# Two score banks in place of the attention's output bank in the first block's output projection

## The chip, the cores and the metric

One NeuronCore of one Trainium2 chip runs the whole program. The metric is device time in microseconds (us) of one execution; the number that counts is the median of several runs. Matmuls accumulate in PSUM, which this kernel uses as eight banks, numbered 0 to 7, each of 128 partitions by 512 float32 values.

## The reference, cut to what matters

Two transformer blocks are applied one after the other to 512 tokens of width 1024, all in float32. The change lies in the first block, and there between these lines:

```python
mixed = jnp.concatenate([out_a.reshape(b, s, A_Q_W), out_b.reshape(b, s, B_W)], axis=-1)
x = x + jnp.einsum('bse,ed->bsd', mixed, w_out)          # the output projection
hn = rmsnorm(x, mlp_norm_g)
hid = jnp.square(jax.nn.relu(jnp.einsum('bsd,df->bsf', hn, w_up)))
x = x + jnp.einsum('bsf,fd->bsd', hid, w_down)
```

`out_a` is a sliding-window attention of eight heads, `out_b` a "forgetting" attention of eight heads; `w_out` is 1024 x 1024, `w_up` 1024 x 4096. The second block (modulation by a conditioning vector, pooling and neighbourhood attention, another MLP) follows.

## The kernel before

**Arithmetic.** Every float32 matrix product is made of three passes over operands that are split into a high and a low part (`split`, lines 149 to 152: ScalarE copies the high part, VectorE subtracts to get the low one; `mm3`, lines 154 to 158: high by high, high by low, low by high). In the profile these are the rows of lines 156, 157 and 158.

**Who sets the order.** The kernel is written in program order, and a scheduler that goes by simulated times makes one fixed list of instructions for each engine from it: an instruction that comes later in the program moves ahead of one whose inputs are late in the simulation. On the chip each engine works through its list in order and waits at the first instruction that is not ready. Tiles of the same tag wait for one another: a new tile in a PSUM bank may be written once the last reader of the tile before it is done.

**Banks.** `banks` (line 146) gives each kind of tile a ring of banks, and `ps` (line 140) hands them out in turn. The first attention has `x=(0, 1)` for projections, `o=(2,)` for the attention's weighted sums, `t=(3, 4, 7)` for transposes and `s=(5, 6)` for scores (line 289). The output projection has `a=A1` and `t=(3, 4)` (line 294), with `A1 = (0, 1, 2)` (line 91). Behind it, line 950 sets `a=(0, 1, 2)`, `t=(3, 4)`, `s=(5, 6, 7)` for the MLP, and line 852 lengthens the ring `s` by `MORE = (0, 1)` until the sixth "up" tile: up tiles 0 to 4 lie in banks 5, 6, 7, 0, 1.

**Attention tail.** `attn_b` (line 666) takes two heads at a time (four pairs). Scores go to a ring `s` bank (lines 676 to 684), VectorE takes the maximum (line 687), ScalarE the exponential (line 689), which is the bank's last reader. The probabilities are transposed (line 707), split, multiplied with the values into bank 2 (`values`, line 712, matmuls of line 581), and `mixed` (line 583) splits bank 2 into `mixT`, the transposed input of the output projection. Counted through the program (1 tile in `gates`, 16 in `attn_a`, 32 in `attn_b`), the ring's last score tile lies in bank 5 and the one before it in bank 6.

**Output projection.** `out_proj` (line 757) goes over two halves of the output columns; in each, `token_major` (line 794) fetches and splits four weight tiles (kp 0 to 3, two k-blocks of 128 each; `o1w00` to `o1w03` for the first half, `o1w10` to `o1w13` for the second) and goes over four token tiles of 128 tokens. Here they are called h0t0 to h0t3 and h1t0 to h1t3. A token tile is 24 matmuls of 128x512 into one bank: 18 for kp 0 to 2 and 6 for kp 3. All token tiles of one kp use the same weight tile, and five weight tiles fit at once (`PARTS = 5`), so `o1w11` takes the place of `o1w00` and can be split only when h0t3 has used that. With three banks in turn, h0t0 to h0t3 are in banks 0, 1, 2, 0 and h1t0 to h1t3 in 1, 2, 0, 1. kp 3 of a token tile is put behind the transposes of the tile two before it (lines 816 and 817).

**After each token tile** `evac1` (line 940) adds the bank to `xa` (line 942, VectorE), multiplies by the norm's gain (`xg`, line 944: GpSimd in the first half, VectorE in the second), transposes on TensorE (line 220; in the trace `n_0t` to `n_3t`), and splits the result into `hT`, the input of the MLP: the first half of the columns makes k 0 to 3 of `hT`, the second k 4 to 7.

**Beside it** `mods` (line 874) computes the second block's modulation rows on VectorE: `macc` (lines 900 and 902, 128x1024 each), fed by 512 KB transfers of `mod`. It begins behind a sigmoid of the conditioning vector, whose exponential (line 883) runs on ScalarE.

**MLP up.** `up` (line 832) makes one 128-wide slice of the hidden layer; for the first five (`NSP = 5`) the 512 tokens go in two halves of 256, each of 24 matmuls (eight k, three passes), so that the first 24 need only the token tiles 0 and 1. Its low weight parts come from GpSimd for the first four slices (`WPJ = 4`).

Of the kernel before, what the change touches and what calls it, by code (L numbers as in the profile page):

```python
# [87 lines left out]
NSP = 5  # L88
MORE = (0, 1)
EARLY = (2, 1)  # L90
A1 = (0, 1, 2)
XR = (3, 5, 7)
A2 = (0, 1, 5, 2, 6)
S2 = (5, 6, 7)
# [39 lines left out]
class Build:  # L134
# [132 lines left out]
    def run(self):  # L267
        tc, nc, a = self.tc, self.nc, self.a
        with ExitStack() as es:
# [21 lines left out]
            with ExitStack() as both:  # L291
                self.xc = both.enter_context(tc.tile_pool(name="xc", bufs=1, reuse_waits="tile"))
                with ExitStack() as ph:
                    self.banks(a=A1, t=(3, 4))
                    self.xp = ph.enter_context(tc.tile_pool(name="xp", bufs=1, reuse_waits="tile"))
# [1255 lines left out]
```

## Time and profile before

| | |
|---|---|
| median of 3 runs | 1253.91 us (1253.65 to 1258.92) |
| the profiled execution's own time | 1258.2 us |
| its span | 1256.4 us |
| busy: TensorE, VectorE, ScalarE, GpSimd | 1211.0, 843.2, 594.2, 256.4 us |
| mean granted TensorE clock | 0.987 |

The span is the profiler's, from the first to the last instruction; the execution's own time is 1.8 us longer. In the profile PE is TensorE, DVE VectorE, ACT ScalarE, POOL GpSimd. A row of a timeline gives start, duration, engine, line, operation, output<-inputs, shape and count, and in brackets how long the engine stood idle before it and what ended that. The duration of a matmul is longer than the spacing to the next one, since matmuls overlap; spacing is what counts. A row of a table of stretches gives for each engine its busy time and number of instructions, then the granted clock as a share of full speed (PEclk), the DMA engines' busy share and GB/s.

The stretch of the change runs from the end of the first attention, at about 230 us, over the output projection to the first "up" slices of the MLP at about 291 us.

### The profile page before, as it was taken

How to read it: one execution, taken by the hardware profiler on the slowest of the kernel's cores; microseconds unless marked ns; L12 is line 12 of the kernel's file. 1: busy time of each engine (PE TensorE's matmuls, PEld its weight loads, DVE VectorE, ACT ScalarE, POOL GpSimd, SP SyncE). 2: the span in 40 equal slices, each digit the busy share in tenths (PEclk: the TensorE clock that was granted, in tenths of full speed). 3: DMA queues.
4: the chain of work that ended last, by engine and by line, in shares of the span. 5: the costliest groups of instructions: out<-in, count | busy, mean ns of one | idle time of the engine just before them, and what ended most of it. 6: DMA issues, size and time to landing. Idle time of an engine off the chain costs nothing. (4 is left out here: it accounts for less than half of the span.)

```text
span 1256.4 us, 16975 instructions
## 1 busy us (share of the span) xinstructions
PE 1211.0 (96%) x6304; PEld 1013.8 (81%) x6304; DVE 843.2 (67%) x1461; ACT 594.2 (47%) x1103; POOL 256.4 (20%) x324
## 2 busy tenths in 40 slices
PE   7899999998999999999999999999899999999997
PEld 6898888788888878888889878777798888888775
DVE  3798776497988864346355557574867568578675
ACT  5576655434323313225245546463566454453442
POOL 2787552243010000000013224030600000000000
PEclk8998999999999999999999999999999999999998
DMA  6221222355668744234145311315355535436331
GB/s 165 64 59 46 66 63 68 101 167 149 206 217 258 235 138 141 67 101 135 67 151 158 85 51 53 102 38 201 119 189 161 166 86 177 142 98 187 101 101 67
DMA packets 154154, 155.42 MB, mean 124 GB/s; under 512 B 14489, under 2 KB 115624, under 8 KB 154072
## 3 DMA queue, kind: packets, MB, share of 16 engines
q1 hardware_dynamic: 149096, 143.08, 37.4%
q0 software_dynamic: 4400, 10.22, 2.6%
q8 instruction: 49, 0.80, 0.3%
q10 hardware_dynamic: 576, 1.05, 0.2%
q14 instruction: 33, 0.27, 0.1%
HBM read 147.96 MB, written 6.36 MB: 123 GB/s over the span
## 5 line engine op out<-in xcount | busy, mean ns | idle before, releaser
L902 DVE SCALAR_TENSOR_TENSOR macc<-mod,silu_c,macc 128x1024 f32<-128x1024 f32 x56 | 76.7, 1379 | 14.1 <-DMA mod<-in_w_mod_dram 14.1
L1453 POOL TENSOR_TENSOR ss<-ss,nhalf 128x1 f32<-128x1 f32 x4 | 3.0, 740 | 332.8 <-DVE ss L1452 332.8
L1305 DVE TENSOR_TENSOR m2d<-m2d,m2d 128x1024 f32<-128x1024 f32 x28 | 34.1, 1222 | 21.9 <-DMA m2d<-in_w_mlp_out_dram 21.8
L979 DVE SCALAR_TENSOR_TENSOR xa<-m1d,r,xa 128x512 f32<-128x512 f32 x32 | 23.8, 746 | 35.3 <-PE m1d L158 35.3
L151 ACT ACTIVATE m1hid<-m1sq 128x512 fp32r<-128x512 f32 x32 | 20.0, 630 | 37.4 <-DVE m1sq L848 37.4
L922 POOL DMA_DIRECT2D modrows<-mrow x8 | 3.9, 492 | 144.4 <-DVE mrow L920 90.2
L152 DVE TENSOR_TENSOR npl<-t,nph 128x512 fp32r<-128x512 f32 x32 | 21.7, 680 | 16.4 <-ACT nph L151 16.3
L152 DVE TENSOR_TENSOR m1hid<-m1sq,m1hid 128x512 fp32r<-128x512 f32 x32 | 21.9, 686 | 9.1 <-ACT m1hid L151 9.1
L185 POOL TENSOR_SCALAR w<-w,g_attn 128x384 f32<-128x384 f32 x20 | 25.6, 1290 | 8.9 <-DMA w<-in_w_in_dram 6.3
L687 DVE TENSOR_REDUCE mb<-sb 128x1 f32<-128x128 f32 (+3 forms) x32 | 15.6, 486 | 16.7 <-PE sb L684 16.6
L198 POOL TENSOR_SCALAR p<-p,d 128x512 f32<-128x512 f32 x8 | 14.0, 1752 | 55.8 <-DVE d L1120 26.5
L1119 ACT ACTIVATE p<-s,m 128x512 f32<-128x512 f32 x32 | 22.0, 689 | 5.8 <-DVE m L1117 5.8
L689 ACT ACTIVATE pb<-sb,mb 128x128 f32<-128x128 f32 (+3 forms) x32 | 16.8, 526 | 15.8 <-DVE mb L687 15.5
L847 ACT ACTIVATE m1re<-m1up 128x512 f32<-128x512 f32 x32 | 18.7, 583 | 11.0 <-PE m1up L158 11.0
L156 PE MATMUL pj<-w_0h,xnT 128*128 128x384 f32 (+1 forms) x48 | 18.5, 386 | 4.5 <-ACT pjs L411 3.3
L151 ACT ACTIVATE nph<-t 128x512 fp32r<-128x512 f32 x32 | 19.1, 596 | 7.4 <-PE t L1130 7.2
L1073 POOL TENSOR_TENSOR tb<-G,nam 128x256 f32<-128x256 f32 x24 | 17.8, 774 | 22.3 <-DVE m L1113 12.5
L848 DVE SCALAR_TENSOR_TENSOR m1sq<-m1up,m1re 128x512 f32<-128x512 f32 x32 | 21.8, 682 | 0.0
L1270 ACT ACTIVATE m2sq<-m2up 128x512 f32<-128x512 f32 x32 | 18.7, 584 | 6.5 <-PE m2up L158 6.5
L1331 DVE TENSOR_TENSOR y<-m2p,y 128x512 f32<-128x512 f32 x32 | 21.1, 682 | 0.2 <-PE m2p L158 0.2
L1272 ACT ACTIVATE m2sq<-m2sq 128x512 f32<-128x512 f32 x32 | 20.2, 633 | 0.9
L151 ACT ACTIVATE pbh<-tb 128x128 fp32r<-128x128 f32 (+3 forms) x32 | 13.7, 435 | 14.5 <-PE tb L707 14.4
(2045 smaller groups left out, 4624.3 us busy)
## 6 DMA issues: line engine op xcount, KB each, us to landing
m2d<-in_w_mlp_out_dram SPq DMA_DIRECT2D x53, 512.0 KB, 3.7
mod<-in_w_mod_dram SPq DMA_DIRECT2D x48, 512.0 KB, 4.4
m1u<-in_w_up_dram SPq DMA_DIRECT2D x32, 512.0 KB, 4.4
m1d<-in_w_down_dram SPq DMA_DIRECT2D x32, 512.0 KB, 3.6
m2u<-in_w_mlp_in_dram SPq DMA_DIRECT2D x32, 512.0 KB, 4.1
w<-in_w_in_dram SPq DMA_DIRECT2D x16, 512.0 KB, 4.0
w<-in_w_in_dram SPq DMA_DIRECT2D x48, 128.0 KB, 2.6
o1w<-in_w_out_dram SPq DMA_DIRECT2D x8, 512.0 KB, 3.7
```

Of the source, the lines that this page charges most:

```text
L151: self.nc.scalar.activation(out=hi, in_=src, func=AF.Copy)
L152: (eng or self.nc.vector).tensor_tensor(out=lo, in0=src, in1=hi.bitcast(F32), op=ALU.subtract)
L185: eng.tensor_scalar(out=rv[:, i], in0=rv[:, i], scalar1=g, scalar2=None, op0=ALU.mult)
L847: ac(out=r, in_=acc, func=AF.Relu)
L848: nc.vector.scalar_tensor_tensor(out=s, in0=acc, scalar=0.0, in1=r, op0=ALU.max, op1=ALU.mult)
L902: nc.vector.scalar_tensor_tensor(out=accs[s], in0=rw, scalar=sc[:, s, k:k + 1], in1=accs[s], op0=ALU.mult, op1=ALU.add)
L979: nc.vector.scalar_tensor_tensor(out=x[t][:, cols], in0=acc, scalar=r2[:, t:t + 1], in1=x[t][:, cols], op0=ALU.mult, op1=ALU.add)
L1119: ac(out=pr, in_=s, func=AF.Exp, bias=m[:, 2:3], accum_out=den[:, 0:1])
L1270: ac(out=s, in_=acc, func=AF.Relu)
L1272: ac(out=s, in_=s, func=AF.Square)
L1305: tt(out=o, in0=x, in1=z, op=ALU.subtract)
L1331: tt(out=Y[n][tau], in0=acc, in1=Y[n][tau], op=ALU.add)
```

## The change

The ring of the first block's output projection is made of the banks 0, 1, 5 and 6, four in place of three. Nothing else is edited. h0t0 to h0t3 then lie in banks 0, 1, 5, 6 and h1t0 to h1t3 in 0, 1, 5, 6 again; bank 2 is not used between the attention's last weighted sum and the MLP. The up tiles stay in banks 5, 6, 7, 0, 1.

```diff
-A1 = (0, 1, 2)
+A1 = (0, 1, 5, 6)
```

## Rows read from the trace of the kernel before

**Rows 1.** The page's busy times: engine, busy us, share of the span, instructions.

```profile
PE 1211.0 (96%) x6304; PEld 1013.8 (81%) x6304; DVE 843.2 (67%) x1461; ACT 594.2 (47%) x1103; POOL 256.4 (20%) x324
```

**Rows 2.** Stretches: busy time by engine, granted clock, DMA share, GB/s.

```profile
core 0: us, PE busy (x) PEld busy (x) DVE busy (x) ACT busy (x) POOL busy (x), PEclk, DMA share, GB/s
230.00:240.00 10.00, 8.90 (x61) 7.12 (x60) 6.64 (x18) 5.48 (x13) 2.03 (x4) 1.00 0.18 55
...
242.00:247.00 5.00, 4.93 (x15) 3.91 (x16) 1.31 (x2) 0.00 (x0) 2.52 (x2) 0.66 1.02 319
247.00:278.00 31.00, 31.00 (x145) 25.18 (x144) 26.11 (x28) 11.55 (x16) 10.44 (x8) 1.00 0.53 161
278.00:291.00 13.00, 9.07 (x58) 8.57 (x58) 13.00 (x12) 4.14 (x6) 12.68 (x8) 0.87 0.62 189
291.00:440.00 149.00, 149.00 (x742) 125.11 (x741) 125.38 (x136) 52.16 (x67) 14.98 (x26) 1.00 0.67 213
```

**Rows 3.** TensorE's waits from 230 to 291 us: us, times, longest.

```profile
PE n_2t L220 <- DVE xg L944: 3.9, 1, 3.9
PE o L156 <- DVE mixT L152: 1.9, 1, 1.9
PE tb L707 <- DVE db L690: 0.9, 1, 0.9
```

**Rows 4.** Timeline of TensorE, 239 to 253 us.

```profile
239.87 0.34 PE L581 MATMUL ob<-pbh,vb3l 128*64 128x128 f32 x2
242.07 0.47 PE L156 MATMUL o<-o1w00h,mixT 128*128 128x512 f32 x1 [1.87 <-DVE mixT L152]
...
247.90 0.39 PE L156 MATMUL o<-o1w00h,mixT 128*128 128x512 f32 x1
...
252.09 0.60 PE L220 MATMUL n_0t<-ident,xg 128*128 128x128 f32 x4
```

**Rows 5.** Timeline of ScalarE, 233 to 252 us.

```profile
233.90 0.69 ACT L689 ACTIVATE pb<-sb,mb 128x512 f32<-128x512 f32 x1
...
249.49 1.06 ACT L151 ACTIVATE o1w11h<-o1w 128x1024 fp32r<-128x1024 f32 x1 [8.01 <-PE o L158]
...
251.86 0.20 ACT L883 ACTIVATE silu_e<-silu_c 128x16 f32<-128x16 f32 x1
```

**Rows 6.** Timeline of VectorE, 250 to 290 us.

```profile
250.59 1.23 DVE L152 TENSOR_TENSOR o1w11l<-o1w,o1w11h 128x1024 fp32r<-128x1024 f32 x1 [7.28 <-ACT o1w11h L151]
...
279.08 0.68 DVE L942 TENSOR_TENSOR xa<-o,xa 128x512 f32<-128x512 f32 x1
279.68 6.31 DVE L902 SCALAR_TENSOR_TENSOR macc<-mod,silu_c,macc 128x1024 f32<-128x1024 f32 x2
285.91 0.68 DVE L944 TENSOR_TENSOR xg<-xa,g_mlp 128x512 f32<-128x512 f32 x1
...
288.91 0.68 DVE L152 TENSOR_TENSOR hT<-n_1t,hT 128x512 fp32r<-128x512 f32 x1
289.51 0.68 DVE L942 TENSOR_TENSOR xa<-o,xa 128x512 f32<-128x512 f32 x1
```

**Rows 7.** Timeline of TensorE, 278 to 291 us.

```profile
278.06 0.28 PE L156 MATMUL m1up<-hT,m1u0h 128*128 128x256 f32 x1
...
282.52 0.29 PE L157 MATMUL m1up<-hT,m1u1h 128*128 128x256 f32 x1
286.74 0.63 PE L220 MATMUL n_2t<-ident,xg 128*128 128x128 f32 x4 [3.93 <-DVE xg L944]
287.12 0.39 PE L158 MATMUL m1up<-hT,m1u1l 128*128 128x256 f32 x1
...
290.85 0.28 PE L157 MATMUL m1up<-hT,m1u0h 128*128 128x256 f32 x1
290.97 0.28 PE L158 MATMUL m1up<-hT,m1u0l 128*128 128x256 f32 x1
```

**Rows 8.** Timeline of GpSimd, 279 to 285 us.

```profile
279.22 2.41 POOL L152 TENSOR_TENSOR m1u1l<-m1u,m1u1h 128x1024 fp32r<-128x1024 f32 x1
281.59 3.32 POOL L152 TENSOR_TENSOR m1u2l<-m1u,m1u2h 128x1024 fp32r<-128x1024 f32 x1
```

**Rows 9.** Instructions writing macc, 256 to 284 us: ns min/median/max, starts, form.

```profile
L902 DVE SCALAR_TENSOR_TENSOR macc<-mod,silu_c,macc x12: 1272/1284/3358, 258.5 to 282.6; 128x1024 f32<-128x1024 f32 x12
```

## The prediction

> **What bounds the kernel now.** I began with the page's busy times: TensorE is busy for 96% of the span [rows 1], so time is only to be had where TensorE waits or where its clock is low. The table of stretches then says where that is. From 291 to 440 us TensorE is busy for all 149 us at full clock [rows 2]: whatever is won or lost before 291 us is carried through that stretch unchanged. From 230 to 291 us there are three losses: a low busy time before 242 us, a granted clock of 0.66 from 242 to 247 us, and 9.07 busy of 13.00 us from 278 to 291 us, at a clock of 0.87 [rows 2]. From 247 to 278 us TensorE is full at full clock.
>
> The list of waits names the gaps: 1.9 us for VectorE's `mixT`, 0.9 us in the last softmax, 3.9 us for `xg` before the transposes `n_2t` [rows 3]. The timeline shows the first of them: after the attention's last weighted sum (matmuls `ob` at 239.87) TensorE stands 1.87 us, until h0t2 begins at 242.07 [rows 4]. That wait is the bank's. h0t2's first 18 matmuls use kp 0 to 2, made of other heads, finished long before; but h0t2 sits in bank 2, and bank 2 still holds the weighted sum that `mixed` reads. h0t3, in bank 0, comes behind it. The clock falls just after this gap, to about half (1.2 of 2.4 GHz): the 18 matmuls of h0t2 take 247.90 - 242.07 = 5.83 us, the next 18, h0t3's, 252.09 - 247.90 = 4.19 us [rows 4].
>
> The last gap has another cause. From 278 to 291 us VectorE is busy for 13.00 of 13.00 us [rows 2]; it is the late engine there, and TensorE fills its time with up slices until 282.52, then waits until 286.74 for `n_2t`, whose input `xg` VectorE began only at 285.91 [rows 6, 7].
>
> **The change part by part.**
>
> *No wait for bank 2.* h0t2 moves to bank 5, h0t3 to bank 6. The last reader of bank 5 is the last exponential, at 233.90 + 0.69 = 234.6 us [rows 5]; bank 6 is free a score tile earlier. So from 234.6 us on h0t2's 18 matmuls, and h0t3's 18, can fill any hole: 36 matmuls at 4.19 / 18 = 0.233 us are 8.4 us of work, more than every hole before 242 us together. Gain: the 1.87 us. The 0.9 us wait in the softmax lies around 234 us, at the edge of the time at which the bank comes free, and whether the scheduler's list has a matmul there isn't to be seen: 0 to 0.9 us, and I take 0.
>
> *The clock.* Without the gap the matmuls behind it should keep the full clock, as they did around the 0.9 us wait: the stretch 230 to 240 us has 8.90 busy of 10.00 and a clock of 1.00 [rows 2]. Gain: 5.83 - 4.19 = 1.64 us; bounds 0 (the clock falls anyway) and 1.64. I take 1.64, for between full busy and a 0.9 us hole no row shows a fall.
>
> The Trainium skill ("TensorE: Matmul & The Clock Gate", section "A second HAM failure mode: psum-queue depth-cycling") blames a falling clock on going round through banks with short pauses. By that rule the 1.64 us would not come back and the gain here would be 1.87 us alone. The trace speaks against it: three banks are gone round from 247 to 278 us at a clock of 1.00 with no hole [rows 2].
>
> *Does it reach the later work?* ScalarE's split of `o1w11` at 249.49 waited 8.01 us for TensorE to be done with `o1w00`, which h0t3 uses last; VectorE's half of that split follows at 250.59 after 7.28 us of idling; and the exponential that lets the `macc` work begin stands in ScalarE's list behind it, at 251.86 [rows 5, 6]. If h0t3's first matmuls come 1.87 + 1.64 = 3.5 us sooner, VectorE's whole dense stretch begins 3.5 us sooner. The DMA engines, at a share of 0.53 from 247 to 278 us [rows 2], have room. So I carry the 3.5 us to VectorE's row at 289.51, where the split of `n_1t` ends and h1t3 can be added: 286.0 us.
>
> *What it costs: the up slices.* Before, up slices 0, 1 and 2 lay in banks 5, 6, 7, free since the attention, and filled TensorE's time while VectorE was late. Now up 0 shares bank 5 with h1t2 (added from 279.08 to 279.8, less 3.5) and up 1 shares bank 6 with h1t3 (added from 289.51, the very end of VectorE's lag) [rows 6]. Up 0 began at 278.06 [rows 7], so it is put off by 1.7 us with work of h1t3 still to be done: nothing. Up 1 is out as a filler. Before 291 us it ran 13 matmuls (8 by 282.52 and 5 after `n_2t`). At full clock an up matmul takes 290.97 - 290.85 = 0.12 us [rows 7], so 13 owed matmuls cost 1.5 us. Bounds: 0, if up 3 and 4 (in banks 0 and 1, long free) come in instead, and 3.1 us, if up 2's 13 are caught behind up 1 as well. I take 1.5, since up 3 and 4 have their weights last.
>
> *What it gives back there.* Before, TensorE was at full speed again at 290.85. It had needed until then for 18 up matmuls at 3.73 / 18 = 0.21 us, at the low clock, from 287.12 on [rows 7], though the input that came next was ready at 289.5 [rows 6]. Without up 1's five it is there when that input is: 3.5 us sooner is 286.0, so 290.85 - 286.0 = 4.8 us sooner, less the 1.5 us owed: 3.3 us.
>
> **The sum:** -3.3 us. Against the profiled execution (span 1256.4, own time 1258.2) that is 1253.1 and 1254.9 us. That execution is 4.3 us above the median of the runs shown, so I put the difference on the median: 1253.9 - 3.3 = 1250.6 us. A measurement of this kernel can tell about 0.5% (6.3 us) from no change, so the forecast counts as no change: 1247.6 and 1260.2 are the edges.
>
> **The rivals.**
>
> *Up 1 as a cork (slower).* TensorE's list is fixed by simulated times, and in it VectorE may be less late than on the chip. If the list has up 1's first matmul ahead of `n_2t`, TensorE stands at it until h1t3 is added, 289.51 + 0.68 - 3.5 = 286.7 us, and the 28 matmuls of up 1, up 2 and up 3 that were done by 290.85 are all owed: 3.4 us, to which the low clock after the longer wait adds as much as it did before, 18 x (0.21 - 0.12) = 1.6 us. TensorE is then where it was at 286.7 + 5.0 = 291.7, that is 0.9 us later than before; with `n_2t`, too, 3.5 us behind its input, the split of `n_2t` and the `xg` of h1t3 follow later on VectorE, up to 3 us more. So 1254.8 to 1258, about 1256. It decides where the cork costs more than the 3.3 us won. For it: up 1 did stand ahead of `n_2t` before (the rows up to 282.52). Against: there its bank was free in the simulation, too; with the bank held, the scheduler knows that it is.
>
> *The collision goes (faster).* Two `macc` instructions take 6.31 us at 279.68, where the usual one takes 1.284 [rows 6, 9]: 3.7 us too many, just ahead of the `xg` that TensorE waits for, and beside two GpSimd splits of 2.41 and 3.32 us [rows 8]. If the new lists put these elsewhere, `xg` comes 3.7 us sooner and the gain is 7.0 us: 1247 us. The Trainium skill ("SBUF — State Buffer", section "Who interferes with whom") has a VectorE instruction with two SBUF inputs and a GpSimd instruction that reads SBUF exclude each other for a whole instruction; the trace agrees in that the pair lasts about as long as two `macc` and the GpSimd rests beside them. For: the lists are made anew. Against: GpSimd and VectorE work hangs on the same chain, so both move together.
>
> *Nothing arrives.* The lists keep h0t2 behind the attention's tail, or VectorE's stretch is held by `mod` transfers and not by `o1w11`: then VectorE ends at the same time and TensorE waits longer for it. 1253 to 1254 us.
>
> **How the numbers follow.** Forecast (the gap and the clock won, up 1 lost), 1249 to 1252.5: 0.50. Cork: 0.18, of which a third for a total beyond 0.5%, where new orders in VectorE's list add another collision of 3.7 us. Collision gone: 0.17, of which three in four beyond 0.5%. Nothing arrives: 0.15. Faster by over 0.5%: 0.13; slower by over 0.5%: 0.06; the same: 0.81. The range reaches from the collision's case with the softmax gap won, too (1246), to the cork's (1257.5).
>
> **What would show it.** Right: in the timeline of TensorE h0t2's matmuls directly behind the `ob` matmuls, or among them, with no wait for `mixT`; a clock of 1.00 from 242 to 247 us; VectorE's split of `o1w11` at about 247 us; up 1's first matmul behind h1t3's addition; TensorE full again from about 287 us. Wrong: a wait of an up matmul for `xa`, of a size like 3.9 us; a clock below 1 in the same place with no gap ahead of it, which would bear out the rule on banks; VectorE still beginning near 250 us; or a change of several us behind 291 us, where nothing is touched and only the order could differ.

## The result: slower, and the profile after

| | before | after |
|---|---|---|
| median | 1254.43 us (5 runs) | 1267.7 us (1264.19 to 1269.83, 5 runs) |
| ratio | | 1.0087, interval 1.0068 to 1.0105 |
| profiled execution, span | 1258.2, 1256.4 us | 1266.07, 1264.3 us |

The forecast was 1250.6 us and "no change". The kernel is slower, by some 11 us after the ratio and by 13.3 us between the medians, with the whole interval above 0.5%.

The page's busy times first, beside [rows 1]:

```profile
PE 1211.1 (96%) x6304; PEld 1013.3 (80%) x6304; DVE 844.5 (67%) x1461; ACT 592.8 (47%) x1103; POOL 255.8 (20%) x324
```

TensorE is busy for the same time to 0.1 us and VectorE to 1.3 us, while the span is 7.9 us longer: by these two profiles the loss is time in which TensorE waits. (Matmuls at a low clock count as busy.) The table of stretches of after (columns as in [rows 2]):

```profile
230.00:240.00 10.00, 10.00 (x58) 8.22 (x58) 4.50 (x11) 4.21 (x10) 0.65 (x1) 1.00 0.17 54
240.00:250.00 10.00, 5.39 (x32) 4.44 (x30) 4.12 (x6) 3.47 (x5) 3.38 (x5) 0.92 0.84 240
250.00:257.00 7.00, 3.78 (x9) 3.00 (x10) 5.55 (x8) 1.16 (x2) 2.51 (x2) 0.50 0.77 258
257.00:278.00 21.00, 21.00 (x98) 17.05 (x97) 17.52 (x16) 5.25 (x8) 7.77 (x4) 0.96 0.40 119
278.00:291.00 13.00, 8.24 (x35) 6.80 (x34) 13.00 (x12) 5.18 (x8) 10.95 (x9) 0.80 0.58 173
291.00:440.00 149.00, 148.29 (x751) 124.56 (x751) 122.56 (x134) 50.27 (x67) 16.92 (x28) 0.99 0.66 202
```

The attention's tail is now full (10.00 busy of 10.00 from 230 us on, where [rows 2] have 8.90), as forecast. What was won there is lost at once: from 240 to 257 us TensorE is busy for 5.39 + 3.78 = 9.2 of 17 us. TensorE's waits from 230 to 300 us of after, beside [rows 3], name the reason:

```profile
PE o L156 <- DVE xa L942: 7.8, 1, 7.8
PE n_1t L220 <- DVE xg L944: 4.8, 1, 4.8
```

The waits for `mixT` and in the softmax are gone, the wait behind the `macc` pair is still there (4.8 us, at `n_1t`, where [rows 3] have 3.9 at `n_2t`), and there is a new one of 7.8 us, of an `o` matmul for an addition. TensorE's timeline in after:

```profile
232.15 0.47 PE L156 MATMUL o<-o1w00h,mixT 128*128 128x512 f32 x1
...
243.76 0.39 PE L158 MATMUL o<-o1w02h,mixT 128*128 128x512 f32 x1
...
245.05 0.34 PE L581 MATMUL ob<-pbh,vb3l 128*64 128x128 f32 x2
253.22 0.79 PE L156 MATMUL o<-o1w10h,mixT 128*128 128x512 f32 x1 [7.83 <-DVE xa L942]
...
258.51 0.44 PE L156 MATMUL o<-o1w12h,mixT 128*128 128x512 f32 x1
```

From 232.15 to 244 us the 36 matmuls of kp 0 to 2 of h0t2 and h0t3 run among the attention's last work. After the last `ob` TensorE has only h1t0 in its list (weights `o1w10`), and h1t0 lies in bank 0, which still holds h0t0. The 12 matmuls behind the wait take 258.51 - 253.22 = 5.29 us, at the lower clock level (1.2 GHz; granted 0.50 from 250 to 257 us); at the spacing of 0.233 us of [rows 4] they would take 2.80.

Why is h0t0's addition late? VectorE's timeline in after:

```profile
243.89 1.23 DVE L152 TENSOR_TENSOR o1w12l<-o1w,o1w12h 128x1024 fp32r<-128x1024 f32 x1 [0.17 <-ACT o1w12h L151]
...
246.69 0.42 DVE L152 TENSOR_TENSOR mixT<-ob,mixT 64x256 fp32r<-64x256 f32 x1 [0.44 <-ACT mixT L151]
251.34 1.23 DVE L152 TENSOR_TENSOR o1w13l<-o1w,o1w13h 128x1024 fp32r<-128x1024 f32 x1 [4.23 <-ACT o1w13h L151]
252.49 1.28 DVE L942 TENSOR_TENSOR xa<-o,xa 128x512 f32<-128x512 f32 x2
...
255.83 1.42 DVE L900 TENSOR_SCALAR macc<-mod,silu_c 128x1024 f32<-128x1024 f32 x2
...
279.50 6.58 DVE L902 SCALAR_TENSOR_TENSOR macc<-mod,silu_c,macc 128x1024 f32<-128x1024 f32 x2
286.01 0.68 DVE L944 TENSOR_TENSOR xg<-xa,g_mlp 128x512 f32<-128x512 f32 x1
```

The additions of h0t0 and h0t1 (252.49, a pair) stand in VectorE's list behind the low split of `o1w13`, the last weight tile of the second half, which h1t0 needs only for its last six matmuls. In before the pair stands directly behind the last `mixT` split, and that weight's split 15 us behind it, in VectorE's timeline of before:

```profile
241.96 1.35 DVE L942 TENSOR_TENSOR xa<-o,xa 128x512 f32<-128x512 f32 x2
...
257.39 1.21 DVE L152 TENSOR_TENSOR o1w13l<-o1w,o1w13h 128x1024 fp32r<-128x1024 f32 x1
```

In after the split waits for ScalarE's, and that for the transfer, in ScalarE's and the DMA queue's timelines of after:

```profile
250.25 1.06 ACT L151 ACTIVATE o1w13h<-o1w 128x1024 fp32r<-128x1024 f32 x1 [3.59 <-DMA o1w<-in_w_out_dram]
```

```profile
243.75 0.37 SPq L173 DMA_DIRECT2D o1w<-in_w_out_dram  x1
```

The transfer goes out at 243.75, when `o1w11`'s buffer is split (VectorE, 242.50 to 243.73), and lands some 6.5 us later. In before the same transfer goes out at 251.84 and ScalarE's split of it begins at 255.57, 3.7 us later; in after it goes out behind loads of `xa`, of which the last lands at 248.2. That these loads slow it down is argued: no run moves them. From 247.1 to 251.3 us VectorE stands, with the inputs of the additions long there, and TensorE stands behind it.

### The profile page after: what moved, and what is told of

Same layout as the page of the kernel before. It is cut to its first block, busy times and chain, and to the rows that moved or that the text cites. A ratio compares the mean times of both kernels' runs of the same rounds, so it can differ in the third digit from the quotient of the medians.

```text
span 1264.3 us, 16986 instructions
## 1 busy us (share of the span) xinstructions
PE 1211.1 (96%) x6304; PEld 1013.3 (80%) x6304; DVE 844.5 (67%) x1461; ACT 592.8 (47%) x1103; POOL 255.8 (20%) x324
## 5 line engine op out<-in xcount | busy, mean ns | idle before, releaser
L151 ACT ACTIVATE mh<-macc 128x1024 fp32r<-128x1024 f32 x8 | 8.5, 1059 | 33.7 <-DVE macc L902 20.8
```

The costliest lines, as they stand in the source:

```text
L151: self.nc.scalar.activation(out=hi, in_=src, func=AF.Copy)
```

## Where the time goes, by stages

Up to the attention's tail the two lists are the same, but single executions arrive there up to 6 us apart, so I set a mark: ScalarE's last `pjs` row (line 411, in the attention; "the attention's last score copy" in an expectation below). From it I take the start of the eighth `m1re` row of line 847 (ScalarE's Relu behind the eighth up slice, "up addend") as the end of the output-projection stage, and eighth to seventeenth as the MLP's first stretch. From the seventeenth to the last it is 130.6 to 131.0 us in all runs from before to e9. Its rows in after:

```profile
202.10 0.58 ACT L411 ACTIVATE pjs<-pj,r 128x384 f32<-128x384 f32 x1
...
339.37 0.60 ACT L847 ACTIVATE m1re<-m1up 128x512 f32<-128x512 f32 x1 [4.92 <-PE m1up L158]
...
489.42 0.58 ACT L847 ACTIVATE m1re<-m1up 128x512 f32<-128x512 f32 x1
```

| profile | mark to eighth | eighth to seventeenth |
|---|---|---|
| before | 130.05 | 147.0 |
| after | 137.27 | 150.05 |
| e8, before again | 126.46 | 149.93 |
| e9, after again | 137.09 | 153.72 |
| e10, e11: before, after without most of the modulation | 130.0, 137.21 | 141.75, 141.83 |
| e12, e13: before, after, modulation at half pace | 125.3, 135.53 | 149.56, 148.54 |
| e1, one split moved | 130.67 | 151.65 |
| e2, e3, e4: other rings | 131.75, 128.38, 127.65 | 151.9, 151.5, 151.92 |
| e5, e6, e7: first `macc` held | 127.73, 132.29, 123.75 | 157.4, 161.2, 156.6 |
| e15, six banks without most of the modulation | 128.01 | 141.58 |
| e14, six banks, modulation at half pace | 126.73 | 149.18 |
| e16, e17: before and six banks, modulation slower in one group | 124.81, 126.48 | 150.59, 149.9 |

So after loses 7 to 11 us in the output-projection stage, depending on which profile of before it is set against, and 3 to 4 us in the MLP's first stretch (150.05 and 153.72 against 147.0 and 149.93).

## The experiments

**Theories.** A: VectorE's list corks TensorE, with h0t0's addition behind `o1w13`'s split. B: the addition itself is late for another reason, its own input. C: the loss is in the transfers and in the banks that the up slices share. Later D and E, on the loss behind the output projection: D, the modulation's `macc` and `mp` rows have new places in the lists; E, it is a late effect of the cork itself.

**e1: the split behind the additions.** The changed kernel, with the scheduler told to issue `o1w13`'s split behind the addition of h0t1:

```diff
+            behind = self.added.get((0, 1)) if (half, kp) == (1, 3) else None
+            with self.tc.issue_after(behind.ins) if behind else nullcontext():
+                return self.weights(f"{name}w{half}{kp}", ...)
```

> The changed kernel (banks 0, 1, 5, 6), with one more rule for VectorE's list: the split of o1w13 may not stand ahead of the additions of h0t0 and h0t1. Theory A (a cork on VectorE: the 7.8 us wait of h1t0 for h0t0's addition is the time that VectorE stands at o1w13's split for that weight's transfer): the addition follows the last split of mixT directly, TensorE's wait of 7.8 us shrinks to about 2.5 us, the low clock behind it lasts shorter, and the time falls by 5 to 9 us against the changed kernel, to 1259 to 1263 us. Theory B (h0t0's addition is late for the load of xa itself, not for the split): the wait stays at 5 us or more and the time stays within 3 us of the changed kernel's 1267.7. Theory C (the loss comes from the order of the transfers, o1w13 and an up weight ahead of mod, or from the up slices' banks): the wait may go, but the time stays at 1265 or more.

1260.93 us against 1256.1, ratio 1.004 (1.0024 to 1.0057), and 6.8 us under after's 1267.7. VectorE's timeline and TensorE's waits in e1:

```profile
242.45 0.42 DVE L152 TENSOR_TENSOR mixT<-ob,mixT 64x256 fp32r<-64x256 f32 x1 [0.44 <-ACT mixT L151]
242.90 1.29 DVE L948 TENSOR_TENSOR xa<-o,xa 128x512 f32<-128x512 f32 x2
247.00 1.23 DVE L152 TENSOR_TENSOR o1w13l<-o1w,o1w13h 128x1024 fp32r<-128x1024 f32 x1 [2.81 <-ACT o1w13h L151]
```

```profile
PE n_1t L220 <- DVE xg L950: 4.7, 1, 4.7
PE o L156 <- DVE xa L948: 2.5, 1, 2.5
```

The additions run directly behind `mixT`, and the wait falls from 7.8 to 2.5 us. The stage is 130.67 us, 6.6 less than after's. A holds for this stage and B falls. But e1 is still 0.4% slower than before: its MLP stretch takes 151.65 us.

**e2, e3, e4: other rings.** Rings without a second half's tile behind an addition that is still owed, or with bank 2 kept:

```diff
-A1 = (0, 1, 5, 6)
+A1 = (0, 1, 5, 6, 7)       # e2
+A1 = (0, 1, 2, 5)          # e3
+A1 = (0, 1, 7, 5, 6, 2)    # e4
```

> The ring is 0, 1, 5, 6, 7: h0t0 to h0t3 lie as in the changed kernel, but h1t0 gets bank 7, free since the attention's transposes, so that it has not to wait for h0t0's addition. Theory A and its base (four banks put h1t0 into h0t0's bank, at a point where TensorE has nothing else): no wait of TensorE for xa between 245 and 253 us; at most some 2.5 us for o1w13's split, which h1t0 needs last; 1256 to 1261 us. Theory C (order of transfers, up slices): no better than 1265.

> The ring is 0, 1, 2, 5: four banks as in the changed kernel, h1t0 in bank 0 as there, but h0t2 stays in bank 2 and so behind the attention's tail. Theory A: 18 matmuls of h0t2 stand between the last weighted sum and h1t0, which gives VectorE's additions 4 us and more, so TensorE's wait for xa is under 2 us, and the wait for mixT ahead of h0t2 is there as in the kernel before (1.9 us). Time within 5 us of the kernel before, 1250 to 1259 us. If four banks as such (h1t0 behind h0t0's addition) cost 10 us wherever the filler stands, 1263 or more.

> The ring is 0, 1, 7, 5, 6, 2: six banks, so that neither h0t2, h0t3 nor h1t0, h1t1 wait for an addition or for mixT to be split, and up slices 0 to 2 get banks that are free early. Theory A: no wait of TensorE over 1 us from 240 to 255 us, full clock there, and the 3.3 us of the prediction or more are won against the kernel before: 1246 to 1252 us. If early fillers are no use because VectorE is late behind them in any case: 1253 to 1256 us, with the waits moved to n_0t or to the up slices.

e2: 1265.58 us, ratio 1.0076 (1.0049 to 1.0102); no wait for `xa`, but h1t0 now comes to the late weight itself and waits 1.7 and 0.8 us for `o1w13`, and the second half's `n_0t` waits 6.0 us for `hT`: other waits take the place of the cork. e3: 1260.97, 1.0052 (1.0033 to 1.0071); the wait for `mixT` (1.9 us) is back, for in this ring h0t2 is in bank 2 again. e4: 1259.86, 1.0033 (1.0018 to 1.0048); TensorE is busy for 17.95 of 18.00 us from 240 to 258 us. All three are slower than before, though e3 and e4 end the stage between the two profiles of before (128.38 and 127.65 us, against 130.05 and 126.46). In e3 h1t0 lies in bank 0 as in after, but 18 of the 36 matmuls stand in front of it again, and no wait for `xa` is left. What is left of the loss is in the MLP stretch, and C, which looked in the output projection's transfers and banks, doesn't tell of it.

**e5, e6, e7: the first `macc` held.** If it is the modulation's place that differs, fix its place: the first `macc` is issued behind h1t3's addition, in before (e5), after (e6) and the six banks (e7).

```diff
+                        with self.tc.issue_after(self.added[1, 3].ins) if cb == 0 else nullcontext():
```

> The kernel before (banks 0, 1, 2), with the first macc instructions held in VectorE's list behind the addition of h1t3, the last of the output projection. It is the base for the next two: from the macc work on, their lists of all engines are the same as this one's. By itself: VectorE is no longer late in the output projection, so the wait of n_2t for xg (3.9 us) should be gone, and 16 macc instructions of 1.3 us, some 21 us, move into the MLP, where VectorE has some 17 us free from 310 to 440 us. 1250 to 1262 us, no theory hangs on it.

> The changed kernel (banks 0, 1, 5, 6) with the same hold. Its lists differ from those of the run before only in the output projection; o1w13's split stands ahead of the additions of h0t0 and h0t1 as in the changed kernel. Theory D (of the 10 us of the change, some 7 are lost in the output projection by the cork, some 3 in the MLP, where the new lists place the macc work otherwise): from the eighth to the 17th up slice both take the same within 1 us, and this kernel is 5 to 8 us slower than the run before, all of it in the output projection. Theory E (the MLP's 3 us are a late effect of the cork itself, transfers out of step or the like): the MLP takes 2 to 4 us more here, too, and the whole is 9 to 12 us slower.

> Six banks (0, 1, 7, 5, 6, 2) with the same hold. Theory D: the early filler is worth what was predicted once nothing corks VectorE and the MLP's lists are those of the base: 2 to 5 us faster than the kernel before with the hold, won before the eighth up slice, with the MLP the same within 1 us. Theory E: the MLP is 2 to 4 us slower as in all rings tried so far, and nothing is won.

1265.04 us (ratio 1.007, 1.005 to 1.009), 1268.9 (1.0103, 1.0081 to 1.0125), 1264.22 (1.0072, 1.0048 to 1.0095). In e6 the wait stands as it was:

```profile
253.14 0.79 PE L156 MATMUL o<-o1w10h,mixT 128*128 128x512 f32 x1 [7.68 <-DVE xa L945]
```

The wait behind the `macc` pair is gone in all three, and e7 has the shortest stage of all (123.75 us), but the modulation then runs late into the MLP and its first stretch takes 157 to 161 us, 8 to 13 more than the mean of before and e8 (in e5 TensorE waits 4.0 us at `mp` for `mh`). After minus before is 4 us timed, 4.6 us in the stage and 3.8 in the MLP stretch by the profiles: this pair doesn't tell D from E.

**e8, e9: both kernels once more.**

> The kernel before once more, for a second profile of the same lists. Both theories: the output-projection stage ends (eighth up addend after the attention's last score copy) within 1.5 us of the first profile's 130.1 us, and the stretch from the eighth to the seventeenth within 0.5 us of its 147.0 us. If the second stretch comes out 3 us apart, then what was read of the mixer's second stage from single profiles is chance, and only the waits of the output projection stand.

> The changed kernel once more. Theory A (TensorE waits in its own list for h0t0's addition, which VectorE's list has behind the last weight's split): the wait of 7.8 us on the third column tile's first matmul is there again, 6 to 9 us, and the eighth up addend comes 5.5 to 9 us later than in the kernel before. The stretch to the seventeenth is 149 to 151 us if what is lost there lies in the lists; as short as before's 147.0 us if it was chance.

One execution of each: 1258.43 and 1273.71 us. The wait of after is repeated (8.1 us), and its stage to 0.2 us. Before's stage is not: 126.46 against 130.05 us. The same gap stands in both profiles of before, with another clock behind it. The stretch from 240 to 245 us, in the first profile of before and then in e8:

```profile
240.00:245.00 5.00, 3.13 (x12) 2.33 (x11) 2.19 (x4) 0.75 (x2) 4.25 (x5) 0.80 0.96 352
```

```profile
240.00:245.00 5.00, 4.17 (x18) 3.46 (x19) 1.76 (x3) 0.23 (x1) 3.28 (x3) 1.00 1.02 354
```

In e8 the h0t2 matmuls behind the 1.87 us wait take 245.09 - 240.83 = 4.26 us, at full clock:

```profile
240.83 0.47 PE L156 MATMUL o<-o1w00h,mixT 128*128 128x512 f32 x1 [1.87 <-DVE mixT L152]
...
245.09 0.39 PE L156 MATMUL o<-o1w00h,mixT 128*128 128x512 f32 x1
```

The MLP stretch varies by 3 us between two profiles of the same lists, so single profiles carry no argument there.

**e10, e11: without most of the modulation.** Column blocks 1 to 5 are left out, and block 0's rows written in their place, so that 48 of the 64 `macc` rows and most `mp` matmuls are gone while the output projection is left almost as it was.

```diff
-        for cb in range(6):
+        for cb in range(1):
```

> The kernel before with the modulation's column blocks 1 to 5 left out (block 0's rows are written in their place, so that part of the computation is missing). It is the partner of the next run: 1235 to 1254 us, since VectorE, GpSimd and the scores' bank lose some 100 us of work that lies beside the mixer's matmuls, and most of that is hidden.

> The changed kernel with the same blocks left out. Theory D (what is lost behind the output projection comes from the modulation's additions and matmuls, whose places in the lists are made anew): the loss left is the output projection's alone, 6 to 8 us over the run before, and the stretch from the eighth to the seventeenth up addend is as long in both, within 1 us. Theory E (the late start of the up projection by itself costs the mixer more, whatever the modulation does): 9 to 12 us over it, with 2 to 4 us of them in that stretch. Theory A's wait of 7 to 8 us on the third column tile stands in both cases.

1247.01 us (ratio to before 0.9944, 0.9921 to 0.9966) and 1253.74 us (0.9981, 0.9963 to 0.9998): after minus before is 6.7 us. By the profiles it is 137.21 - 130.0 = 7.2 us in the stage and 141.83 - 141.75 = 0.1 us in the MLP. The stretch from the eighth to the seventeenth addend of e10, then of e11 (TensorE alone: length, busy, granted clock):

```profile
330.09:471.84 141.75, 141.75 (x611) 1.00 0.29 86
```

```profile
340.67:482.50 141.83, 141.83 (x611) 1.00 0.28 86
```

and with the modulation, before and then e9:

```profile
333.75:480.75 147.00, 145.81 (x627) 1.00 0.65 208
```

```profile
339.34:493.06 153.72, 149.22 (x626) 0.98 0.65 200
```

Without the modulation TensorE never waits there, in either kernel. With it the stretch has 24 `mp` matmuls and, by the records, 8 others fewer: 16 more, 16 x 0.23 = 3.7 us, and 141.75 + 3.7 = 145.4 is close to before's 145.81 busy. The rest is waits and the clock after them: 1.2 us idle in before, 2.0 in e8, 3.5 in after, 4.5 in e9. E falls: a late start by itself costs the MLP nothing. What after loses in the MLP hangs on the modulation, as D has it; that it is the new places of its rows is argued, since these runs take the rows out and do not move them.

**e12, e13, e14, e15: slower pace, and six banks.** One step of the modulation per up slice or down addition in place of two (before, after, six banks); e15 is the six banks without blocks 1 to 5.

```diff
         def extra(grp):
-            next(gen, None)
+            if grp == 3:
+                next(gen, None)
```

> The kernel before with one step of the modulation per up tile or down addition in place of two, so that its additions and matmuls spread over about twice as many of the mixer's matmuls. If the modulation's pace is what makes the stretch from the eighth to the seventeenth up addend scatter (147.0 and 149.9 us in two profiles of the kernel before, 141.8 us without most of it), this kernel's stretch is shorter, 143 to 147 us, and the later stretches longer by 0 to 4 us: 1250 to 1257 us in all.

> The changed kernel with the same slower pace. Theory D (beyond the wait on the third column tile, the change loses only through the modulation's places in the lists): 6 to 8 us over the run before, nearly all of it ahead of the eighth up addend, as in the pair without the modulation. If what is lost in the mixer stays (10 us or more over the run before), the pace isn't what does it and Theory D holds only in that leaving the modulation out hides the loss.

> The ring of six banks (0, 1, 7, 5, 6, 2) with the slower pace: the version that the experiments point to. With the six banks no tile of the second half takes a bank whose addition is still owed, so the eighth up addend comes 2 us earlier than in the kernel before (127.7 against 130.1 us), and the pace takes the mixer's loss away: 1249 to 1254 us, 1 to 3 us under the run of the kernel before with the same pace, where that is the theory; 2 to 4 us over it where the six banks cost the mixer something that has nothing to do with the modulation.

> The ring of six banks with the modulation's column blocks 1 to 5 left out (block 0's rows in their place, so that part of the computation is missing). It shows what a rotation is worth that has no tile behind an owed addition: 1 to 4 us under the kernel before with the same blocks left out (1247.0 us), all ahead of the eighth up addend; not under it if filling the early holes only moves the wait to the transposes of the second half.

e12: 1267.75 us, ratio 1.0087 (1.0067 to 1.0106); e13: 1274.81, 1.0143 (1.0122 to 1.0165); e14: 1266.97, 1.0078 (1.0056 to 1.01). The pace is no gain: the last block of the modulation is drained in the last group, and the context rows behind it come late, in e12:

```profile
PE nc_0t L220 <- DVE nc_0x L236: 6.0, 1, 6.0
```

From the seventeenth to the last addend e12 takes 142.1 us, e13 141.1. But the pair tells what it was for: e13 minus e12 is 7.1 us, and the MLP stretch of the changed kernel is not longer (148.54 against 149.56). That agrees with the pair without the modulation (6.7 us). The profiles put 10.2 us into the stage, 1 us of it given back in each of the two later stretches.

e15: 1244.55 us, ratio to before 0.9904 (0.9885 to 0.9922), that is 2.5 us under e10 with the stage 2.0 us shorter (128.01 against 130.0). That does not show that filling the holes is worth 2 us. Each of the two has an interval of about 2.5 us to either side, and e10's profile is one with the low clock behind the 1.87 us gap (granted 0.74 from 240 to 245 us). Where before's list ran there at full clock, the stage of the six banks is the longer one: e14 126.73 against e12's 125.3, e17 126.48 against e16's 124.81. New waits take the place of the old one: in e4, e14, e15 and e17 an up matmul waits 2.1 to 2.2 us for `xa` and another 2.0 to 2.3 us for `hT`.

**e16, e17: slower pace in the first group alone.**

```diff
-            next(gen, None)
+            if grp:
+                next(gen, None)
```

> The kernel before with the slower pace (one step of the modulation per call) in the mixer's first group alone, so that the modulation is through before the last group, whose context transposes cost the all-slow pace 6.0 us of TensorE and some 11 us between the seventeenth and the last up addend. If the pace in the first group is worth anything by itself, the stretch from the eighth to the seventeenth up addend falls under 147 us and the run comes to 1250 to 1255 us; if not, 1255 to 1260 us.

> The ring of six banks with the slower pace in the first group alone. Without the modulation this ring was 2.5 us under the kernel before, with it 3.6 us over. If the pace in the first group takes that loss away, this one is 1 to 4 us under its partner and may be under the kernel before (1250 to 1254 us); if the modulation's additions cost the six banks their gain wherever they stand, it is 2 to 5 us over its partner.

1253.8 us (ratio 0.999, 0.9977 to 1.0003) and 1254.3 us (0.9996, 0.9985 to 1.0006). The six banks' loss of 3.3 in 1000 (e4) is gone, but no gain is to be measured, and no version that does the whole computation beats before. In both TensorE still waits at `mp` for `mh` (2.6 and 2.3 us).

## Why the prediction was wrong, point by point

**The step that failed** is the price in "What it costs". It looks at the banks 5 and 6 alone and asks 1.5 us; that h1t0 has to wait for h0t0's addition in bank 0 is put at nothing, without a reason. There the runs show 7.8 us of waiting and 2.5 us of low clock. The step ahead of it, that the 3.5 us won are carried to VectorE's whole stretch, failed too. The points in the prediction's order:

**No wait for bank 2: right.** The 1.87 us are gone, and so is the 0.9 us wait in the softmax, which I had put at 0 to 0.9. TensorE's stretch from 230 to 240 us is full.

**The clock: the mechanism was right, the size a matter of chance.** With no gap the clock is 1.00 from 230 us to the last `ob` (5.00 busy of 5.00 at 1.00 from 240 to 245 us, too). But the 1.64 us were no fixed cost of before: in e8, e12 and e16, behind the same 1.87 us gap, the clock stays at 1.00; in the first profile of before, in e5 and in e10 it falls. I had read a chance of one execution as a term of the kernel. The rule of the Trainium skill on going round through banks ("TensorE: Matmul & The Clock Gate", section "A second HAM failure mode: psum-queue depth-cycling") is not borne out by after either: its falls between 230 and 300 us stand behind the two waits of 7.8 and 4.8 us.

**"Does it reach the later work?": here the prediction failed first.** ScalarE's split of `o1w11` did come 8 us sooner (241.40, where [rows 5] have 249.49; 6.5 us when both are set against the mark). I carried that to VectorE's whole stretch. But VectorE's first `macc` began at 255.83, not sooner than before (254.94), for in the new list `o1w13`'s split stands in front of the additions and the sigmoid, and its transfer can't land before 250 us.

**"What it costs: the up slices": the cost was looked for at the wrong tile.** I went through the banks 5 and 6 that the up slices share with h1t2 and h1t3, and left out banks 0 and 1. A ring of four brings h1t0 back to bank 0. In before h1t0 also needed a bank that waited for an addition (h0t1's, bank 1), but VectorE ran that directly behind the last `mixT` split, and the 36 matmuls of h0t2 and h0t3 lay in front of h1t0, 5.83 + 4.19 us [rows 4], and covered it. I counted these 36 as filler for the early holes, "more than every hole", and did not ask what they had been covering where they stood. Moved forward by 10 us (8.3 against the mark), they leave that place bare. e1 parts the wait: with the addition directly behind `mixT` again 2.5 us are left, so the other 5.3 of 7.8 us are `o1w13`'s split in front of it. Together that is 7.83 us of waiting and 2.5 us of low clock, against 1.87 + 0.9 us and, where the clock fell, 1.64 us won. That is 10.3 - 4.4 = 5.9 us on the first profile of before and 10.3 - 2.8 = 7.5 us on one without the fall; the stage lost 7.2 and 10.8. The rest lies behind it, at the wait of 4.8 us and its low clock (granted 0.86 from 290 to 300 us, where before has 0.96).

**"What it gives back there": nothing came back.** VectorE's stretch did not begin sooner, and the wait for `xg` is 4.8 us in place of 3.9. The low clock behind it, which the 4.8 us of the prediction count in, was no fixed cost either: from 278 to 291 us it is 0.87 in the first profile of before and 1.00 in e8.

**The cork: right in kind, wrong in place.** No up matmul waits for `xa` before 291 us. A matmul that the fixed list puts first and whose bank is not free is what happened, but at h1t0, some 33 us earlier, with a price of 10 us and not the 3.4 + 1.6 us of the rival. (In the ring of six banks an up matmul does wait for `xa`, 2.2 us in e4.) That the scheduler took the addition to be done by then is argued from its choice of order; no run shows its simulated times.

**The collision: no change, as in the forecast.** The `macc` pair takes 6.58 us (279.50), beside two GpSimd splits:

```profile
279.33 2.39 POOL L152 TENSOR_TENSOR m1u1l<-m1u,m1u1h 128x1024 fp32r<-128x1024 f32 x1
281.69 3.31 POOL L152 TENSOR_TENSOR m1u2l<-m1u,m1u2h 128x1024 fp32r<-128x1024 f32 x1
```

These are the figures of [rows 6, 8] to 0.3 us, so "both move together" was right. With the wait of 4.8 us that follows, the last transposes of the stage come at 300.23 us, where before has 293.47.

**"Carried through that stretch unchanged": wrong by 3 to 4 us.** From 291 to 440 us before's TensorE had no idle time [rows 2], and I took the order there as given. The modulation is interleaved with the MLP by the same scheduler. From the eighth to the seventeenth addend TensorE waits for a down addition on VectorE (at `m1d`) or for the split of `macc` (at `mp`): 1.2 us in the first profile of before, 2.0 in e8, 3.5 and 4.5 in the two of after, and not at all without most of the modulation.

**The range.** Its upper end, 1257.5 us, was the cork at up 1; after lies 10 us above. No case was priced in which the filler's old cover was needed.

## What to carry to other kernels

A tile that is moved forward to fill a hole is cover taken from the place where it stood: name the wait that it had been hiding there, and who releases it, before the hole is counted as won. When a ring of buffers is made longer, write down for every later tile whose release it now waits for, and look in the releasing engine's list for an instruction in front of that release that waits for a transfer. And take a second profile of the same kernel before a clock row becomes a term of a sum.

## What the runs showed of the hardware that was not expected

The same wait of TensorE, 1.87 us at the same place, was followed by the lower clock level in three profiles (before, e5, e10: granted 0.80, 0.71 and 0.74 from 240 to 245 us) and by full clock in three others (e8, e12, e16: 1.00); in e3, where h0t2 waits as long in another list, it was full clock too (1.00 from 245 to 250 us). The 7.6 to 8.1 us waits were followed by the lower level in every one of five profiles (after, e6, e9, e11, e13): 9 to 12 matmuls at a spacing of 0.43 us before it returned to 0.23.
